# Nearest-neighbour upsampling by 2: the first store with 55 rows copied by one engine instead of 54 by two

## Chip, cores and metric

The kernel runs on one core of a Trainium2 chip. The metric is the device time in microseconds of one execution. Before the change the median of three runs is 197.02 us (196.93 to 197.18).

## What is computed

The input has 16 x 64 images of 64 x 64 float32; every pixel is written four times, as a 2 x 2 block of an image of 128 x 128. Nothing is computed: it is a copy that makes four words of one.

```
result = np.zeros((batch, channels, 2 * h, 2 * w), dtype=np.float32)
for i in range(new_h):
    for j in range(new_w):
        result[:, :, i, j] = x[:, :, i // 2, j // 2]
```

The input is 16.8 MB, the output 67.1 MB.

## The kernel before

All 16 x 64 x 64 = 65,536 input rows are dealt to 128 partitions, 512 rows (of 64 words) each. One input row becomes two output rows of 128 words, so 256 words (1 KiB) of output on its partition.

There is one big buffer, `mem` (line 187), of 52,992 words on each partition. The input stands in its upper part, `xt` (line 188), which begins at word 20,224; the 20,224 words ahead of it are free at first.

SP, the engine that issues all transfers here, first issues three loads (line 195): rows 0 to 32, rows 32 to 288, rows 288 to 512. A helper moves them ahead of the barrier at the start of the program, and another one (`close_early`) rearranges the end; neither is touched by the change.

Then nine stores follow, with the numbers of rows in the list `rows` (line 181). For each of them (lines 204 to 216) the rows are expanded into a buffer `u` inside `mem`, by two engines at once: VectorE copies the first `kv` rows (line 213), ScalarE the rest (line 214), both from the same access pattern `expanded`, in which each word is read twice and each row twice (steps of 0). Then SP issues the store (line 215). For the first store `kv` is all rows but one (53 of 54); for the others it is about five eighths of the rows, made even (line 212).

The buffers alternate (line 206): stores 0, 2, 4, 6 and 8 use the words from 0 on; stores 1, 3, 5 and 7 use a region that ends where the rows still to be expanded begin, and so overwrites input that is used up. Within each of the two kinds a store's copies may begin only when the transfer that last read these words has landed. I number the stores 0 to 8.

The order on each engine is that of the loop: VectorE has nine copies in a row, ScalarE a table load and nine copies, SP three loads and nine stores. All transfers go through one queue, and are dealt to 16 DMA engines, 8 partitions each, one packet for a partition's rows. The waits are set by the framework, from the words that instructions read and write: each copy waits for the loads it reads, and for the stores that still read the words that it overwrites; each store waits for its copies.

Of the kernel before, what the change touches and what calls it, by code (L numbers as in the profile page):

```python
# [153 lines left out]
@with_exitstack  # L154
def kernel(
    ctx: ExitStack,
    tc: tile.TileContext,
    x: bass.AP,
    scale_factor: int,
    out: bass.AP,  # L160
):
    nc = tc.nc
    nc.at_finalize(begin_before_barrier)
    nc.at_finalize(close_early)
    P = nc.NUM_PARTITIONS
    s = int(scale_factor)
    B, C, H, W = x.shape
    R = B * C * H // P
    fdt = x.dtype

    xp = x.rearrange("b c h w -> (b c h) w").rearrange("(p r) w -> p r w", p=P)
    op = out.rearrange("b c (h hd) w -> (b c h) (hd w)", hd=s).rearrange(
        "(p r) w -> p r w", p=P
    )

    rows = [54, 38, 54, 61, 54, 63, 63, 63, 62]
    GROW = s * s
    FREE = 79
    WF = FREE * GROW * W
    assert sum(rows) == R
    mem_pool = ctx.enter_context(tc.tile_pool(name="mem", bufs=1))
    mem = mem_pool.tile([P, WF + R * W], fdt, name="mem")
    xt = mem[:, WF:].rearrange("p (r w) -> p r w", r=R)

    HEAD = 32
    cuts = [0, HEAD, R // 2 + HEAD, R]
    for lo, hi in zip(cuts, cuts[1:]):
        nc.sync.dma_start(out=xt[:, lo:hi], in_=xp[:, lo:hi])  # L195

    def expanded(r0, r1):
        return (
            xt[:, r0:r1].unsqueeze(2).unsqueeze(4).to_broadcast([P, r1 - r0, s, W, s])
        )  # L200

    r0 = 0
    before = (0, 0)
    for n, k in enumerate(rows):
        size = k * GROW * W
        at = 0 if n % 2 == 0 else WF + r0 * W - size
        assert at >= before[1] or at + size <= before[0]
        before = (at, at + size)
        u = mem[:, at : at + size].rearrange(
            "p (k a w b) -> p k a w b", k=k, a=s, w=W  # L210
        )
        kv = k - 1 if n == 0 else k * 5 // 8 & ~1
        nc.vector.tensor_copy(out=u[:, :kv], in_=expanded(r0, r0 + kv))  # L213
        nc.scalar.copy(out=u[:, kv:], in_=expanded(r0 + kv, r0 + k))  # L214
        nc.sync.dma_start(out=op[:, r0 : r0 + k, :], in_=u)  # L215
        r0 += k

# [34 lines left out]
```

## Time and profile before

| what | value |
|---|---|
| median of three runs | 197.02 us (196.93 to 197.18) |
| the profiled execution | 196.92 us |
| its span, first to last instruction | 195.6 us |
| VectorE busy | 52.3 us in 9 copies |
| ScalarE busy | 42.1 us in 9 copies and a table load |
| moved by DMA | 83.89 MB in 1728 packets, 429 GB/s over the span |

The profile comes from one execution, whose span is 1.3 us shorter than its time. Times in views of the trace count from the start of the span. In the rows of instructions, a copy's shape is partitions x output words, so 256 words are one input row. "DVE" is VectorE, "ACT" ScalarE, "SPq" SP's queue.

The chain of work that ended last goes, by its shares, 65% through transfers, 11% through ScalarE's copies and 7% through VectorE's. It follows each store back to the copy that fed it and the landing that this copy waited for, so it names copies also where other transfers were under way beside them. Some landings are wanted below, by the ends of waits in the trace: load 2 near 24.0 us, store 0 at 57.30, store 1 at 68.89, store 2 at 85.09, store 3 near 103.6, store 4 at 119.82.

### The profile page before, as it was taken

The page shows a single profiled execution, that of the slowest core. Times are in us where ns is not written, and L with a number is a line of the kernel's source. Part 1 is how long each engine was busy: PE and PEld are TensorE (multiplying, and loading weights), DVE is VectorE, ACT ScalarE, POOL GpSimd, SP SyncE. Part 2 cuts the span into 40 slices and gives each one's busy share as a digit, 9 for nine tenths or more (in the row PEclk, how much of TensorE's full clock was granted, in tenths as well). Part 3 has the DMA queues.
Part 4 walks back from the last instruction along what each step waited for, and adds up shares of the span by engine and source line. Part 5 has one row for each costly group of instructions (what it writes and reads, how often), then busy time and mean ns, then how long its engine had stood idle before and what let it go on. Part 6 is the DMA issues. An engine that isn't in the chain of part 4 may idle for free.

```text
span 195.6 us, 102 instructions
## 1 busy us (share of the span) xinstructions
DVE 52.3 (27%) x9; ACT 42.1 (21%) x10; POOL 0.2 (0%) x4
## 2 busy tenths in 40 slices
DVE  0000099940026091053008204500540073000000
ACT  2000000160029700059500004970000073000000
POOL 0000000000000000000000000000000000000000
DMA  9999989889899989999999899999999999999994
GB/s 429 429 429 429 402 375 563 375 362 543 362 436 390 555 362 418 486 409 409 409 420 532 362 531 433 422 422 422 422 422 422 422 422 422 422 435 545 467 428 208
DMA packets 1728, 83.89 MB, mean 429 GB/s; under 512 B 192, under 2 KB 192, under 8 KB 192
## 3 DMA queue, kind: packets, MB, share of 16 engines
q1 hardware_dynamic: 1728, 83.89, 99.2%
HBM read 16.78 MB, written 67.11 MB: 429 GB/s over the span
## 4 chain that ended last, share of the span: by engine, by line
DMA 65%; ACT 11%; DVE 7%; SPq 0%; issue 0%; DVEq 0%; ACTq 0%
DMA out_dram<-mem 53%; DMA mem<-in_x_dram 12%; ACT mem L214 11%; DVE mem L213 7%; SPq L195 0%; DVEq L213 0%; ACTq L214 0%; SPq L215 0%
## 5 line engine op out<-in xcount | busy, mean ns | idle before, releaser
L213 DVE COPY mem<-mem 128x9728 f32<-128x9728 f32 (+3 forms) x9 | 52.3, 5818 | 110.9 <-DMA out_dram<-mem 86.8
L214 ACT COPY mem<-mem 128x6400 f32<-128x6400 f32 (+5 forms) x9 | 40.8, 4530 | 119.4 <-DMA out_dram<-mem 84.2
L214 ACT ACT_TABLE_LOAD x1 | 1.3, 1283 | 1.7 <-PEq L233 1.7
L233 POOL MEMSET const-bfloat16-1.0<- 128x1 bf16 x1 | 0.1, 102 | 0.0
L233 POOL MEMSET const-uint8-127<- 128x1 uint8 x1 | 0.1, 102 | 0.0
L233 POOL MEMSET const-float32-1.0<- 128x1 f32 x1 | 0.1, 99 | 0.0
L233 POOL MEMSET const-float32-0.0<- 128x1 f32 x1 | 0.1, 98 | 0.2 <-issue 0.2
## 6 DMA issues: line engine op xcount, KB each, us to landing
out_dram<-mem SPq DMA_DIRECT2D x3, 8064.0 KB, 32.4
out_dram<-mem SPq DMA_DIRECT2D x3, 6912.0 KB, 22.9
out_dram<-mem SPq DMA_DIRECT2D x1, 7936.0 KB, 32.3
out_dram<-mem SPq DMA_DIRECT2D x1, 7808.0 KB, 29.3
mem<-in_x_dram SPq DMA_DIRECT2D x1, 7168.0 KB, 40.1
out_dram<-mem SPq DMA_DIRECT2D x1, 4864.0 KB, 26.7
mem<-in_x_dram SPq DMA_DIRECT2D x1, 1024.0 KB, 4.7
mem<-in_x_dram SPq DMA_DIRECT2D x1, 23.6
```

Of the source, the lines that this page charges most:

```text
L213: nc.vector.tensor_copy(out=u[:, :kv], in_=expanded(r0, r0 + kv))
L214: nc.scalar.copy(out=u[:, kv:], in_=expanded(r0 + kv, r0 + k))
L233: nc = _bacc.Bacc("TRN2", target_bir_lowering=False, num_devices=1)
```

## The change

The first store has 55 rows, all copied by VectorE in one instruction; ScalarE has no copy for it. The second has 37 rows instead of 38. The later sizes are 54, 61, 54, 62, 63, 63, 63 instead of 54, 61, 54, 63, 63, 63, 62.

```diff
-    rows = [54, 38, 54, 61, 54, 63, 63, 63, 62]
+    rows = [55, 37, 54, 61, 54, 62, 63, 63, 63]
...
-        kv = k - 1 if n == 0 else k * 5 // 8 & ~1
+        kv = k if n == 0 else k * 5 // 8 & ~1
         nc.vector.tensor_copy(out=u[:, :kv], in_=expanded(r0, r0 + kv))
-        nc.scalar.copy(out=u[:, kv:], in_=expanded(r0 + kv, r0 + k))
+        if kv < k:
+            nc.scalar.copy(out=u[:, kv:], in_=expanded(r0 + kv, r0 + k))
```

The order of the instructions on each engine stays the same but for the one copy that ScalarE no longer has. Two waits change. SP's first store waits for VectorE alone; and since store 1's buffer now lies in words 14,272 to 23,744 instead of 13,952 to 23,680, ScalarE's copy for store 3, which writes words 23,680 to 29,568, overlaps it and waits for store 1 to land. ScalarE's table load, which had no wait, now carries the wait for loads 1 and 2 that its first copy had.

## The prediction

> **What bounds the kernel now.** I read the page's header, busy times and queue table first.
>
> ```profile
> span 195.6 us, 102 instructions
> ...
> DVE 52.3 (27%) x9; ACT 42.1 (21%) x10; POOL 0.2 (0%) x4
> ...
> DMA  9999989889899989999999899999999999999994
> ...
> q1 hardware_dynamic: 1728, 83.89, 99.2%
> HBM read 16.78 MB, written 67.11 MB: 429 GB/s over the span
> ```
>
> One queue, 16 DMA engines, 99.2% of their time filled; VectorE and ScalarE idle three quarters of theirs. The change moves no byte out of the kernel (512 rows are loaded and 512 stored either way), so its time can only move where a DMA engine runs dry, or where a packet takes longer. The place to look is the first hand-over, from loads to stores. The timeline, by windows, has it:
>
> ```profile
> 24.03 0.41 ACT L214 COPY mem<-mem 128x256 f32<-128x256 f32 x1 [21.03 <-DMA mem<-in_x_dram]
> 24.11 14.29 DVE L213 COPY mem<-mem 128x13568 f32<-128x13568 f32 x1 [24.11 <-DMA mem<-in_x_dram]
> ...
> 38.48 3.61 ACT L214 COPY mem<-mem 128x4096 f32<-128x4096 f32 x1 [14.04 <-DVE mem L213]
> 38.48 3.97 SPq L215 DMA_DIRECT2D out_dram<-mem  x2
> ```
>
> The first store is issued at 38.48 us, 0.07 us after VectorE's copy ends at 24.11 + 14.29 = 38.40. ScalarE's row was ready at 24.44. When do the DMA engines need that store? The table by stretches of the trace, with its last two columns DMA share and GB/s (a packet is counted whole where it starts, so shares over 1 occur):
>
> ```profile
> 1.00:1.10 0.10, 0.00 (x0) 0.00 (x0) 0.00 (x0) 1.00 2.42 492
> ...
> 1.00:1.50 0.50, 0.00 (x0) 0.00 (x0) 0.00 (x0) 1.00 1.26 262
> ...
> 37.90:38.50 0.60, 0.60 (x2) 0.02 (x1) 0.00 (x0) 1.00 3.56 1529
> ...
> 40.00:40.10 0.10, 0.10 (x1) 0.10 (x1) 0.00 (x0) 1.00 1.28 553
> ...
> 40.20:40.30 0.10, 0.10 (x1) 0.10 (x1) 0.00 (x0) 1.00 6.41 2765
> ...
> 40.60:40.70 0.10, 0.10 (x1) 0.10 (x1) 0.00 (x0) 1.00 1.28 553
> ...
> 192.40:193.00 0.60, 0.00 (x0) 0.00 (x0) 0.00 (x0) 1.00 3.90 1693
> ```
>
> From 37.9 to 38.5, 1529 GB/s x 0.6 us = 917 KB start: the 16 last packets of load 3 (224 rows are 57,344 B on each of 8 partitions per engine). They take 3.56 x 0.6 x 16 / 16 = 2.1 us each, so they end at 40.0 to 40.6. The first packets of store 0 (55,296 B) start from 40.0 to 40.7: one engine in the first tenth, five in the third, one in the last. No gap shows: the store was there in time. How early is read from load 1, the only transfer that met an empty queue: issued at 0.00, its 16 first packets (8192 B; 262 GB/s x 0.5 us = 131 KB) start from 1.00 to 1.50, six of them before 1.10. So store 0, issued at 38.48, was ready at about 39.5 to 40.0: an estimated half microsecond ahead of need. That cover is what the change spends.
>
> **The change part by part.**
>
> *VectorE copies 55 rows instead of 53.* The copies' rows by shape:
>
> ```profile
> L213 DVE COPY mem<-mem 128x9728 f32<-128x9728 f32 x5 | 26.1, 5227 | 59.7 <-DMA out_dram<-mem 59.7
> ...
> L213 DVE COPY mem<-mem 128x13568 f32<-128x13568 f32 x1 | 14.3, 14285 | 24.1 <-DMA mem<-in_x_dram 24.1
> ...
> L213 DVE COPY mem<-mem 128x8192 f32<-128x8192 f32 x2 | 8.9, 4428 | 27.1 <-DMA out_dram<-mem 27.1
> ...
> L213 DVE COPY mem<-mem 128x5632 f32<-128x5632 f32 x1 | 3.1, 3083 | 0.0
> ```
>
> 38, 32 and 22 rows run at 0.54 to 0.55 ns an element, 53 rows at 1.05: half the rate. 53 is the only odd count, and also the longest copy; 55 is odd and longer, so both readings leave it at half rate. That loads were landing meanwhile is not the reason: the 22-row copy ran at full rate from 38.4 to 41.5, beside the end of load 3. The slope at full rate is (5227 - 4428) / 1536 = 0.520 ns an element, at half rate 1.040, so 512 more elements cost +0.53 us: 14.82 us, ending near 38.94.
>
> The Trainium skill (VectorE: DVE Perf Modes, What auto-detection actually checks) gives an fp32 copy two elements a cycle when the outermost counts of source and destination are both even, or equal. Taken as the code writes its views, 53 equals 53 and 55 equals 55, and both would be fast; the measured 14.29 us speaks against that reading, unless the contiguous destination counts as one long run. By the fast reading the sum's first term would be -6.7 us instead of +0.53, which is a rival below.
>
> *ScalarE's one-row copy goes (0.41 us).* It ran at 24.03, beside VectorE's 14.29 us: worth nothing. With it goes one of the two semaphores that SP waits for ahead of store 0; VectorE's is the last, and between its end and the issue lie 0.07 us, of which I let -0.05 to 0 go. ScalarE's table load (1.28 us) now waits for loads 1 and 2 in the instruction order and moves from 1.72 to about 24; behind it stands only the copy for store 1, not due before 39: 13 us of cover, and only beyond that would it count.
>
> *So store 0 is issued at about 39.01 instead of 38.48* and, by load 1's spread, ready on the engines from 40.01 to 40.51. By rank against their need (six ready by 40.11, where three are needed by 40.20; the last two by 40.51, where the last two are needed in 40.50 to 40.70) nobody waits. By the worst pairing, the last engine served is the first one free: 0.5 us idle. An engine that restarts from empty may also take longer over its first packet. The trace shows no store that meets an empty engine. From below: store 0's first packets follow load 3's with no gap, 0. From above: load 1's first 16 packets take 1.26 x 0.5 x 16 / 16 = 0.63 us, where 8192 B at the queue's steady rate (435 GB/s over 16 engines) take 0.30: +0.33. Both ends stay in the range; I take the sum of wait and restart as 0.1 us, near the lower end, because the pairing by rank is the natural one (engines that began first should end first) and because not every engine's loss shows: the last packets of the last store start from 192.4 to 193.0, and an engine that is not the last to end can lose up to this spread, some 0.4 us, for nothing.
>
> *Store 0 has 55 rows, store 1 has 37.* Together 92 as before. Store 0 takes one row longer, (57.30 - 40.3) / 54 = 0.31 us, so it lands near 57.6, and store 1 where it did. ScalarE's share of store 1 is 3840 instead of 4096 elements: at the slope (5525 - 3606) / 2304 = 0.83 ns, 0.21 us less; it ends near 42.4 instead of 42.1. Store 1 is due when store 0 ends, near 57: 14 us of cover. The copies for store 2 wait for store 0's landing, start 0.3 us later and end near 62.5, with store 1's transfer lasting until 68.9: some 5 us left after 1.0 to 1.5 us from issue to first packet.
>
> *One wait is added.* Store 1's buffer now begins at word 14,272 and ends at 23,744, 64 words into ScalarE's part of store 3's buffer (from 23,680). ScalarE's 5888-element copy, which ran at 62.2, must wait for store 1's landing at 68.89, as VectorE's copy for that store did already. It ends at 68.9 + 5.1 = 74.0, beside VectorE's end at 74.1, so store 3 is issued when it was; it is due at 85, when store 2 ends. Queued behind it on ScalarE is the copy for store 4, which waits for store 2's landing at 85.1 anyway. Cost 0 while these 10 us stand.
>
> *Store 5 has 62 rows and store 8 has 63.* ScalarE gets 6144 elements for the first (-0.21 us) and 6400 for the last (+0.23). The last copy runs 157.86 to 163.4, its store is due at 176: no cost. The bytes and the 12 transfers stay, so the rate does.
>
> Sum against the profiled execution (196.92 us, of which 195.6 is the span and 1.3 lies around it): +0.53 of delay, less the half microsecond of cover, leaves +0.1, or 197.0. That execution is 0.1 below the median of the runs; on the median I say **197.1**.
>
> **The rivals.**
> 1. *The store comes too late (slower).* Engines run dry at 40.0 to 40.6 and refill slowly. Price: up to 0.5 wait + 0.33 restart, 197.4 to 197.85. It decides from the point where the engine that ends last waits over 0.3 us. For it: 0.53 us of delay against an estimated half microsecond of cover, which comes from a load at the start, not from a store. Against: pairing by rank, and the spread at the end. Chance 0.29.
> 2. *The 55-row copy runs at full rate.* 14,080 x 0.537 = 7.6 us, store 0 issued near 31.8, 8 us ahead. DMA is full either way: 197.0. Against it: the 53-row row. Chance 0.05, inside no change.
> 3. *A better hand-over (faster).* If the engines ended together instead of over 0.4 us, 0.3 us would go: 196.7. Nothing in the change aims there, and the 16 engines' shares stay equal. Below that the bytes stand in the way. Chance 0.07.
>
> **How the numbers follow.** Forecast (cover just holds, 197.0 to 197.4) 0.59, with rival 2 0.64 for within 0.2%; slower 0.29, faster 0.07. A measurement of this kernel can tell about 0.2%, 0.4 us, from no change. Range 196.75 to 197.8: the repeats of before go down to 196.93, the upper end takes in nearly the whole price of rival 1.
>
> **What would show it.** The first copy at 14.8 us and store 0 issued near 39.0; in stretches of 0.1 us, first packets of store 0 from 40.0 to 40.7 as before (cover held) or bunched at 40.5 to 41 (rival 1), with load 3's last packets starting at 37.9 to 38.5. Store 0 landing at 57.6, store 1 at 68.9; later than 69.2 means rival 1. My account would be wrong if a gap between packets showed anywhere else, or if the first packets came later than 1.0 to 1.5 us after issue.

## The result and the profile after

The changed kernel takes 197.58 us (median of 10 runs, 197.35 to 197.70) against 197.08 us (10 runs, 196.88 to 197.33): a ratio of 1.0024 with a 95% interval of 1.0015 to 1.0034, so 0.5 us slower. That lies in the range of the prediction, 0.5 us above its number and just outside what I had called no change. Within the range it is by luck: the upper end had been stretched for a rival, and what the forecast said would happen (the cover just holds) did not.

The page of after, header and DMA:

```profile
span 196.3 us, 100 instructions
...
DMA  9999989889898989999999899999999999999994
...
q1 hardware_dynamic: 1728, 83.89, 99.1%
```

The queue looks as full as before: nothing of 0.5 us can be seen at this grain. The timeline of after around the hand-over, and the first ScalarE copies behind it:

```profile
24.16 1.28 ACT L215 ACT_TABLE_LOAD   x1 [24.16 <-DMA mem<-in_x_dram]
24.16 17.82 DVE L213 COPY mem<-mem 128x14080 f32<-128x14080 f32 x2 [24.16 <-DMA mem<-in_x_dram]
39.01 124.98 SPq L216 DMA_DIRECT2D out_dram<-mem  x9
39.02 3.39 ACT L215 COPY mem<-mem 128x3840 f32<-128x3840 f32 x1 [13.58 <-DVE mem L213]
...
69.17 5.10 ACT L215 COPY mem<-mem 128x5888 f32<-128x5888 f32 x1 [6.42 <-DMA out_dram<-mem]
```

and the row of the long copy:

```profile
L213 DVE COPY mem<-mem 128x14080 f32<-128x14080 f32 x1 | 14.8, 14821 | 24.2 <-DMA mem<-in_x_dram 24.2
```

The copy takes 14.82 us and store 0 is issued at 39.01, both as worked out. The other movements are there too, and each is still covered. The hand-over is not. These are stretches of the trace of after; the last two columns are DMA share and GB/s, and a packet counts whole where it starts:

```profile
37.90:38.65 0.75, 0.75 (x1) 0.00 (x0) 0.00 (x0) 1.00 2.82 1223
40.00:40.40 0.40, 0.40 (x1) 0.40 (x1) 0.00 (x0) 1.00 1.67 704
40.40:40.80 0.40, 0.40 (x1) 0.40 (x1) 0.00 (x0) 1.00 3.65 1549
```

and the same of before:

```profile
37.90:38.65 0.75, 0.75 (x2) 0.17 (x1) 0.00 (x0) 1.00 2.85 1223
40.00:40.40 0.40, 0.40 (x1) 0.40 (x1) 0.00 (x0) 1.00 4.17 1797
40.40:40.80 0.40, 0.40 (x1) 0.40 (x1) 0.00 (x0) 1.00 0.96 415
```

In the first stretch start the last load packets, 1223 x 0.75 = 917 KB, 16 packets in both. In before, 1797 x 0.4 / 55.3 KB = 13 of 16 engines have begun on store 0 by 40.4; in after 704 x 0.4 / 56.3 KB = 5. The packet records behind these views give the gap. They do not name the engine; where a packet starts within 4 ns of another one's end, I take the two as one engine's. In before each of the 16 last load packets has such a successor. In after only one has; the other 15 engines wait. Which of their starts belongs to which end the records do not say, but the mean needs no pairing: 0.16 us over all 16, 0.17 over the 15. The mean engine begins store 0 at 40.45 instead of 40.32.

That is 0.13 us. The rest comes later, as the chain of work that ended last shows; first after, then before:

```profile
39.01 18.83 DMA out_dram<-mem
...
125.93 32.15 DMA out_dram<-mem
```

```profile
38.48 18.82 DMA out_dram<-mem
...
125.45 32.39 DMA out_dram<-mem
```

Store 0 lands at 39.01 + 18.83 = 57.84, store 6 at 125.93 + 32.15 = 158.08: 331 rows in 100.24 us, 0.3028 us a row. Before: 57.30 to 157.84, 333 rows in 100.54 us, 0.3019. In the mean a row is stored 0.3% slower, and the records show no gap between packets there. In the packet records a packet of 63 rows takes 2.385 us where it took 2.380, one of 54 rows 2.046 instead of 2.041, and from start to start it is some 6 ns more for the same rows. Over the 71 packets that follow an engine's first, with 0.04 us for the first one, this is 0.47 us: from an engine's first store packet to its last end, 155.08 us in the mean instead of 154.61. The one engine that did not wait goes at the fast pace for 34 packets and then, from about 107 us on, shows the longer packets too, without a gap ahead of them. So the two profiles differ by 0.13 at the hand-over, 0.47 in the pace, and the rest of their 0.67 us in how the 16 engines' ends spread. (The profiled execution of before was 0.16 us below the median of its ten runs; the medians differ by 0.50.)

### The profile page after: what moved, and what is told of

Read it like the earlier page. It is cut to its first block, busy times and chain, and to the rows that moved or that the text cites. A ratio compares the mean times of both kernels' runs of the same rounds, so it can differ in the third digit from the quotient of the medians.

```text
span 196.3 us, 100 instructions
## 1 busy us (share of the span) xinstructions
DVE 52.8 (27%) x9; ACT 41.4 (21%) x9; POOL 0.2 (0%) x4
## 4 chain that ended last, share of the span: by engine, by line
DMA 65%; ACT 11%; DVE 8%; SPq 0%; issue 0%; DVEq 0%; ACTq 0%
DMA out_dram<-mem 53%; DMA mem<-in_x_dram 12%; ACT mem L215 11%; DVE mem L213 8%; SPq L195 0%; DVEq L213 0%; ACTq L215 0%
## 5 line engine op out<-in xcount | busy, mean ns | idle before, releaser
L215 ACT COPY mem<-mem 128x6400 f32<-128x6400 f32 (+4 forms) x8 | 40.2, 5019 | 98.0 <-DMA out_dram<-mem 84.4
```

## The experiments

Two readings were open. **L**: store 0 is issued too late. **S**: the new sizes or moved buffers make transfers slower. A ratio is against the kernel before, timed on the same chip beside the runs of a group; its median was 197.2 us beside the first four, 197.5 beside the next four and 197.4 beside the last four, so times of different groups are not compared.

### Four runs to part lateness from sizes

**Sizes of after, issue of before** (an edit of the changed kernel).

```diff
-        kv = k if n == 0 else k * 5 // 8 & ~1
+        kv = k - 2 if n == 0 else k * 5 // 8 & ~1
```

> All sizes as after (55, 37, ... 62, 63, 63, 63), but in the first store VectorE copies 53 rows and ScalarE the other 2, so that store 0 is issued near 38.5 us again. Theory L (lateness: what counts is when store 0 is issued): 197.1 us, ratio 1.000 against before. Rival S (sizes: packets of 55, 37 and 62 rows, their order or the moved buffers make the transfers slower): as after, 197.6, ratio 1.0024.

Measured: ratio 1.000 (0.9991 to 1.0008), store 0 issued at 38.48, no engine dry, packets of 63 rows 2.380 us again. S falls: with all the new sizes and buffers, two rows handed back to ScalarE undo the whole loss.

**Sizes of before, issue a little later.**

```diff
-        nc.scalar.copy(out=u[:, kv:], in_=expanded(r0 + kv, r0 + k))
+        if n == 0:
+            nc.vector.tensor_copy(out=u[:, kv:], in_=expanded(r0 + kv, r0 + k))
+        else:
+            nc.scalar.copy(out=u[:, kv:], in_=expanded(r0 + kv, r0 + k))
```

> All sizes as before, but VectorE copies the 54th row too, in a second instruction behind the one of 53 rows (about 0.4 us), so that store 0 is issued near 38.9. Theory L: slower by most of that delay, 197.4 to 197.5, ratio 1.0015 to 1.002, with 54 rows. Rival S: as before, 1.000.

Measured: 1.0002 (0.9993 to 1.0011). The second copy cost only 0.21 us behind the first, so store 0 went at 38.67, not 38.9, and the test was weaker than meant. Its trace stands between: 3 of the 16 engines run dry, and just these 3 then show the longer packets to the end; their last packets end 0.27 us or more behind those of the other 13. The time as a whole does not tell it from before.

**54 rows in one even instruction.**

```diff
-    rows = [55, 37, 54, 61, 54, 62, 63, 63, 63]
+    rows = [54, 38, 54, 61, 54, 63, 63, 63, 62]
```

(on the changed kernel, so `kv = k = 54`)

> All sizes as before, the first 54 rows all by VectorE in one instruction: an even count. If the half rate comes from the odd count, the copy takes 13,824 x 0.537 = 7.4 us and store 0 is issued near 31.6; by theory L the cover was already enough, so 197.1, ratio 1.000, at most 0.1 us less. If the half rate comes from the length, the copy takes 14.55 us, store 0 is issued near 38.7 and the time is near 197.2 to 197.3. Rival S: 1.000.

Measured: the copy takes 7.37 us, so it is the odd count that halves the rate, not the length. But the time is **slower**, ratio 1.0068 (1.0055 to 1.0081). Here L, by which early is safe, falls. The chain and the stretches of this run:

```profile
24.06 7.37 DVE mem L213
...
31.45 27.54 DMA out_dram<-mem
```

```profile
37.90:38.65 0.75, 0.00 (x0) 0.00 (x0) 0.00 (x0) 1.00 4.95 1223
40.00:40.40 0.40, 0.00 (x0) 0.00 (x0) 0.00 (x0) 1.00 0.00 0
...
41.60:42.40 0.80, 0.00 (x0) 0.00 (x0) 0.00 (x0) 1.00 2.56 1106
```

The same 16 last load packets start at the same time, but take 4.95 x 0.75 = 3.71 us instead of 2.85 x 0.75 = 2.14. No copy is running on either engine meanwhile (the zeros in these rows), so copies beside them are not the reason. All load packets ahead of them take 2.12 to 2.13 as before. Store 0 then begins 1.55 us late, and goes on at the fast pace.

**57 rows** (an edit of the changed kernel).

```diff
-    rows = [55, 37, 54, 61, 54, 62, 63, 63, 63]
+    rows = [57, 35, 54, 61, 54, 62, 63, 63, 63]
```

> As after, with 57 rows in the first store and 35 in the second: another 512 elements at half rate, copy 15.35 us, store 0 issued near 39.5. Theory L: now no cover is left, so each further 0.53 us counts in full: 198.1, ratio 1.005, with first packets of store 0 near 41 us. Rival S: no more than after, 197.6, ratio 1.0024, since bytes and packets per engine are the same in number.

Measured: 1.0021 (1.0012 to 1.0030), no more than after. Issued 0.43 us later than in after, its engines restart from 40.49 to 40.78, against 40.19 to 40.77: the last one no later. So the first half microsecond of lateness had already cost nearly all that this one costs: a step, not a slope. Both share the pace, 155.10 and 155.08 us from first store packet to end, and nearly the gap, 0.21 and 0.16 us in the mean.

### How early is too early, and what the step is

The next three runs shift work from VectorE to ScalarE in the first store (`kv = 45`, `49`, `51` of 54 rows, all odd), the sizes being those of before.

```diff
-        kv = k - 1 if n == 0 else k * 5 // 8 & ~1
+        kv = 45 if n == 0 else k * 5 // 8 & ~1
```

> Sizes as before; of the first 54 rows VectorE copies 45 (odd, so at half rate: 45 x 256 x 1.04 ns + 0.17 = 12.15 us) and ScalarE 9, so store 0 is issued near 36.3 us and ready on the engines from 37.3 to 37.8, before the last packets of load 3 start (37.9 to 38.4). Theory P (a store that is already queued when the last load packet starts makes that packet 1.6 us longer, as all 16 were in the run with the store at 31.5): 198.4 to 198.5, ratio 1.0065, nearly all last packets near 3.7 us. Rival G (the loss grows with the lead, 7 us of lead for 1.6): lead 2.2 us more than before, 197.6, ratio 1.0025. Rival F (the loss comes from the full-rate copy, not from the early store): 1.000.

Measured: 1.0037 (1.0024 to 1.0051). F falls, for the copy took 12.16 us, at half rate.

> As the run with 45 rows, with 49 for VectorE (13.22 us) and 5 for ScalarE: store 0 issued near 37.35, ready from 38.35 to 38.85, behind the start of most last load packets. Theory P: as before, ratio 1.000, a few long last packets at most. Rival G: 197.35, ratio 1.001.

Measured: 1.0026 (1.0017 to 1.0034), where P had said 1.000.

> As the run with 45 rows, with 51 for VectorE (13.75 us) and 3 for ScalarE: store 0 issued near 37.9, ready from 38.9 to 39.4, between the two losses. Theory P: no long packet and a full microsecond of cover before the engines run dry, so 197.0 to 197.1 in every run, ratio 0.9995, at best 0.998 if before itself runs dry on an engine in some executions. Rival G: 197.25, ratio 1.0005.

Measured: 0.9998 (0.9989 to 1.0007).

The first stretch, with the 16 last load packets, of the runs with 45, 49 and 51 rows, one fence each:

```profile
37.90:38.65 0.75, 0.75 (x1) 0.75 (x1) 0.00 (x0) 1.00 4.32 1223
```

```profile
37.90:38.65 0.75, 0.75 (x1) 0.75 (x1) 0.00 (x0) 1.00 3.75 1223
```

```profile
37.90:38.65 0.75, 0.75 (x2) 0.59 (x1) 0.00 (x0) 1.00 3.00 1223
```

Times 0.75, the packets take 3.24, 2.81 and 2.25 us. With the issue of store 0: 31.45 gives 3.71, 36.48 gives 3.24, 37.56 gives 2.81, 38.06 gives 2.25, 38.48 gives 2.14, and from 38.67 on 2.12. So the loss grows with the lead, as G says, but not evenly: half of it comes within the last microsecond and a half. P's threshold is not there. In all three no engine runs dry and a packet of 63 rows takes 2.380 us. By the packets the losses are 1.1, 0.7 and 0.1 us; the ratios show less, I take it because the kernel before, which they are held against, ran dry itself in some executions (its times go from 197.02 to 197.69 us, and the next run shows such a hand-over).

**A late store in the middle.** In the kernel before, store 6 is expanded late: VectorE copies 9 of its rows twice and all 63 by itself.

```diff
+        if n == 6:
+            kv = k
+            nc.vector.tensor_copy(out=u[:, :9], in_=expanded(r0, r0 + 9))
         nc.vector.tensor_copy(out=u[:, :kv], in_=expanded(r0, r0 + kv))
-        nc.scalar.copy(out=u[:, kv:], in_=expanded(r0 + kv, r0 + k))
+        if kv < k:
+            nc.scalar.copy(out=u[:, kv:], in_=expanded(r0 + kv, r0 + k))
```

> Before, but the copy of store 6 is made late on purpose: VectorE copies 9 of its rows twice and all 63 in one odd instruction (2.6 + 17.0 us from 119.9), so its store is issued near 139.4 and its first packets start near 140.4 to 141, after the engines run dry at 138.2 to 138.9. Theory R (an engine that restarts from empty on a store takes some 5 to 7 ns longer for every packet from then on): from store 6 on a row takes 0.303 us instead of 0.302, packets of 63 rows near 2.386 us instead of 2.380, and the end comes at before + gap of about 2 us + 24 x 7 ns = 0.17 us. Rival (the longer packets of after come from something else than the restart): packets as before, 2.380 us, after the gap.

Measured: 199.71 us in one execution, 2.2 above the median of before beside it, as expected. Up to store 6 this is the kernel before, and in this execution load 2 landed late and store 0 was issued at 38.87: 11 of the 16 engines ran dry at the hand-over and showed long packets from the first store on, and 5 went on without a gap, with short ones. The chain around the gap:

```profile
90.41 29.89 DMA out_dram<-mem
...
123.05 16.96 DVE mem L216
...
140.03 20.45 DMA out_dram<-mem
```

Between store 5's last packets and the first of store 6 every engine waits about 2 us. From there on all 16 show the long packets, 2.387 us for 63 rows (median), those five too. So a restart brings on the longer packets, and nothing in the first store is needed: theory R holds. It is not shown to be the only way, since one engine of after went over without a gap.

### Further out, another queue, and repeats

**59 rows.** `rows = [59, 33, 54, 61, 54, 62, 63, 63, 63]`.

> As after, with 59 rows in the first store and 33 in the second: copy 15.9 us, store 0 issued near 40.0, first packets from 41.0 to 41.5. Theory D (running dry costs a step once, by the slower packets that follow, and from there on the wait itself one for one): 0.53 us more than with 57 rows, whose ratio was 1.0021, so 198.05 to 198.15 by a before of 197.1, ratio 1.0048. Rival (the step is all; lateness itself is free up to here): 1.0022.

Measured: 1.0032 (1.002 to 1.0045); D's number was 1.0048. The chain and stretches of this run:

```profile
24.42 15.90 DVE mem L213
...
40.33 19.28 DMA out_dram<-mem
```

```profile
40.40:40.80 0.40, 0.40 (x1) 0.40 (x1) 0.00 (x0) 1.00 0.02 0
40.80:41.20 0.40, 0.40 (x1) 0.40 (x1) 0.00 (x0) 1.00 2.12 906
41.20:41.60 0.40, 0.40 (x1) 0.40 (x1) 0.00 (x0) 1.00 3.55 1510
```

Now every engine is idle when the store arrives, and all begin between 41.18 and 41.33, 0.85 to 1.00 us after the issue. In this execution the mean gap is 0.66 us, and the last end is 0.33 us behind that of the repeat of after below: lateness counts from here on. In the mean of the 16 ends it counts one for one (0.49 us later than the repeat, by a mean gap of 0.66 instead of 0.18); the last end moves less, because engines that restart together also end together (within 0.2 us instead of 0.6). Part of the missing ratio may lie in the before timed beside it, whose repeat below ran dry on one engine itself.

**The early store on ScalarE's queue** (an edit of the run with the even 54 rows).

```diff
-        nc.sync.dma_start(out=op[:, r0 : r0 + k, :], in_=u)
+        queue = nc.scalar if n == 0 else nc.sync
+        queue.dma_start(out=op[:, r0 : r0 + k, :], in_=u)
```

> As the run with 54 rows by VectorE in one even instruction (store 0 ready at 31.5, ratio 1.0068), but store 0 is issued from ScalarE's queue instead of SP's. Theory Q (the loss of the early store lies in a store packet queued behind a load packet of the same queue): here the engines take packets of both queues in turn from 32.5 on, no last load packet of 3.7 us, ratio 1.000. Rival (it lies in any change from loads to stores with the store ready, or mixing both directions costs too): ratio 1.004 or more.

Measured: 201.84 us, ratio 1.0225 (1.0211 to 1.0239). The time alone does not part Q from its rival: store 0, sharing the engines with load 3 and then store 1, lands at 67.02 instead of at 58.99 as in the run with the even 54, so the copies for store 2 start there and store 2 is issued at 71.95, after store 1 has ended at 70.85. A second dry stretch, of its own making, adds to the time. But the stretches of this run show the load packets ahead of store 0:

```profile
31.90:32.35 0.45, 0.45 (x1) 0.18 (x1) 0.00 (x0) 1.00 4.73 2039
34.00:34.45 0.45, 0.45 (x1) 0.45 (x1) 0.00 (x0) 1.00 7.20 2039
37.10:37.90 0.80, 0.00 (x0) 0.00 (x0) 0.00 (x0) 1.00 2.77 1106
```

In each of the first two, 2039 x 0.45 = 918 KB start, 16 load packets; in the third the 16 first packets of store 0. The load packets that start 0.2 to 0.6 us after the issue at 31.71 take 4.73 x 0.45 = 2.13 us, the next ones, right ahead of the store, 7.20 x 0.45 = 3.24. So the longer load packet is there although the store stands in another queue: in this Q falls. What makes the packet longer stays open.

**Repeats, for their traces.**

> The changed kernel once more, for its trace: if what was read of one execution is a property of the kernel, store 0's first packets start some 0.1 to 0.5 us behind the end of load 3's again, and a row takes 0.3028 us from store 0's landing to store 6's, not 0.3019.

Measured: 197.84 us; all 16 engines run dry (mean gap 0.18 us); store 0 lands at 58.08 and store 6 at 158.36, 331 rows at 0.3030 us.

> The kernel before once more, for its trace: 0.3019 us a row where no engine ran dry at the hand-over; where some did (load 2 landing late moves the issue of store 0 past 38.5), between that and 0.3028.

Measured: 197.31 us. The chain:

```profile
24.33 14.30 DVE mem L213
...
38.70 18.79 DMA out_dram<-mem
```

Load 2 lands 0.2 us later here than in the first profile, store 0 goes at 38.70, and one of 16 engines waits, 0.18 us. That engine alone shows the longer packets all the way, and it ends last, 0.26 us behind the next; the row takes 0.3022 us. Before itself stands on the edge, and in some executions steps over it.

## Why the prediction was right and wrong

The prediction named the right place, and put more weight on the wrong one of its two cases there: the cover did not hold.

- *The work moved* came out step by step: copy 14.82 us (14.82 predicted), issue 39.01 (39.01), the table load at 24.16 and ScalarE's wait for store 1 at 69.17, both still covered. The copies and issues behind the first store cost nothing.
- *The half rate* belongs to the odd count: 54 rows took 7.37 us, 55 rows 14.82. The Trainium skill (VectorE: DVE Perf Modes, What auto-detection actually checks) asks for even or equal outermost counts; the traces fit it if the contiguous destination does not count as 53 or 55 rows, which no run here shows.
- *"A half microsecond ahead of need"*, the cover, was the step that failed first. I read it from load 1, which met an idle queue, and paired engines by rank: ready 1.0 to 1.5 us after the issue. With 59 rows, where all engines had run empty, the first packets did start 0.85 to 1.00 us after the issue. In after every load packet ended 1.04 us or more after the issue, and yet 15 of 16 engines waited where I had none waiting. The wait is about the same whenever there is one: 0.17 to 0.21 us in the mean of the engines that waited, for issues from 38.67 to 39.44. That the mean shift, 0.13 us, is close to the 0.1 in my sum is a coincidence.
- *"Longer over its first packet"* was the term that failed in kind. I bounded a restart at 0 to 0.33 us, once. Measured, the first packet of a restarted engine is only some 0.04 us longer, but every packet after it takes some 6 ns more too: over 71 of them, 0.43 us, with the first 0.47 us. That is most of the 0.67 us between the two profiles. Store 6 held back, the two runs of after and the 57 and 59 rows show it; the runs in which no engine waited have none of it.
- *"Not every engine's loss shows"* did not help: nearly all engines slowed alike, so the last end went with them; and in the repeat of before a single slow engine ended last.
- *Rival 1* named the mechanism (engines run dry) and 197.4 to 197.85 us; the result, 197.58, is inside, by a wait of 0.16 instead of 0.5 us and a pace that it did not have. By its own condition, a wait of over 0.3 us on the engine that ends last, it would not have decided. The sign that I named for it, store 1 landing later than 69.2 us, missed it too: the copies that wait for this landing start at 69.17 and 69.19.
- *Rival 2* ("DMA is full either way: 197.0") was wrong for the case it describes: with the store 7 us ahead the time is 198.5. Being early is no free cover here.

What causes the two losses inside a DMA engine is not shown. The Trainium skill (DMA: Bandwidth & Descriptors, Two DMAs through the same engine are not ordered) says that an engine starts the descriptors of a queue in order, but pipelined, with separate read and write sides; a store whose read goes on beside the last load's write would fit the longer last packet of one queue, and no run here tells whether it is so.

No run was faster than before: issues from 38.06 to 38.67 us give ratios of 0.9998 to 1.0002.

## What to carry to other kernels

A queue that is 99% busy can still be slowed from its edges: look at the hand-over from loads to stores packet by packet, and count whether each engine goes on without a gap. Cover has two ends, so try the issue both earlier and later before calling it safe. And a stall need not be paid once: compare the pace behind it (us per row between landings) with the pace of a run that had none.

## What the runs showed of the hardware

- A DMA engine that ran dry ahead of a store kept a slower pace for the rest of the program: 2.385 us instead of 2.380 us for a packet of 64,512 B, seen engine by engine within one execution (1, 3 or 11 of 16 dry, and the same ones slow), and set off on the 5 still fast ones by one forced gap of 2 us. One engine of after took on the slow pace without a gap.
- A store that is ready early lengthens the load packet right ahead of it. With the lead counted from the issue to the time at which the load's first engine would end by packets of 2.12 us: 2.12 us at a lead of 1.4 us, 2.81 at 2.8, 3.24 at 3.9, 3.71 at 8.6. With the store on another queue it was 3.24 us.
- From issue to a store's first packets it took 0.85 to 1.00 us on engines that had run empty, 1.05 to 1.8 us (57 rows and the two runs of after) on engines that had just finished a load; these stood idle for about 0.2 us in between.
